# An encoder block in float32 on one core: the first two tiles side by side, first weights of a stage split earlier, first output products paired

## The chip, the cores and the metric

The kernel runs on one core of a Trainium2 chip. A core has TensorE (PE in the profile: matrix products into PSUM banks of 128 x 512 float32), VectorE (DVE), ScalarE (ACT), GpSimd (POOL), and SyncE (SP), which here issues the transfers between the chip's memory and SBUF. The engines run their instructions each in its own order and wait for one another through semaphores. The metric is the device time of one execution in microseconds, lower is better.

## The reference

One layer of a bidirectional encoder for two groups of sequences, 512 and 2048 tokens of width 1024, with 16 meta tokens in front of each:

```python
def mixer_layer(h, norm_g, w_in, na_rpb, sink, w_proj_a, w_proj_b, w_out, t5_bias):
    u = rms_norm(h, norm_g)
    proj = u @ w_in
    qa, ka, va, za, qb, kb, vb, zb, ga, gb = jnp.split(proj, cuts, axis=-1)
    o_a = neighbourhood_attention(qa, ka, va, na_rpb, n)
    o_b = window_attention(qb, kb, vb, t5_bias, sink, n)
    y_a = (o_a * jax.nn.silu(za)) @ w_proj_a
    y_b = (o_b * jax.nn.silu(zb)) @ w_proj_b
    merged = jax.nn.sigmoid(ga) * y_a + jax.nn.sigmoid(gb) * y_b
    return merged @ w_out
...
    h = h + mixer_layer(h, ...)
    return rms_norm(h[:, N_META:], final_g)
```

Branch a attends to a neighbourhood on a grid of 64 columns (8 heads of 64), branch b to a window of 128 tokens to either side (8 query heads, 2 key heads). Everything is float32.

## The kernel before

The 2560 tokens are five windows of 512: window 0 is the short sequence, 1 to 4 the long one. Activations lie feature-major, 128 features by 512 tokens to a tile. A float32 operand is split in a high and a low part (`split_part`: ACT copies the high part, then DVE or POOL subtracts for the low one), and a product is three products of parts (`mm3`, L135 to L137). Which engine makes the low part of weights is set by `lo_eng`: DVE in the first stages, POOL during attention.

The input projection has 42 output tiles of 128 features and 8 tiles of input (KT = 8), so 24 products to a tile and window. It runs in stages:

1. `beside(firsts, ...)`: the last window alone, 18 tiles one after another. `alone` runs one tile, `project` its products, with a yield after every six. `prep_last` first loads this window's x in four transfers of two tiles, scales it by the norm's weight (u, high part on ACT at L313, low on DVE at L314), squares it (L316) and adds up the squares (rs, L318 and L321). Its next step, which makes the reciprocal root, is called at the 9th and 14th yield. Meanwhile `prep_first` prepares windows 0 and 1, by a list of yields at which its steps are called (its sums rsp at L402, fin_v at L407).
2. `pass_(0, ...)` with `pairs`: windows 0 and 1 together, two tiles of weights at a time, by a scheme with seven products instead of eight (L758).
3. `beside(rest, ...)`: further tiles of the last window alone.
4. `pass_(2, ...)`: windows 2 and 3 as in 2.
5. Attention. Each window has 32 units of branch a, then 16 of branch b (`unit_a`, `unit_b`), cut into steps by yields. A b unit handles two heads: scores s, maximum, exponentials prs, normalising, transposes tp, products with v (ob). Between the steps TensorE's order is filled up with dense steps of six products by `fill`, with an account (`due`) that says how many are owed. The dense work of a window, in this order: `dense_pa` (psa, from y of branch a), `dense_pb` (psb, from y of branch b), `dense_out` (the output projection of w_o, whose results are hT), `dense_fin` (the final norm's factor rbs, and hT times rbs on POOL, L1239). psb of window w comes in the a units of window w + 1.
6. `finish_end`, for the last window: psb in pairs of tiles, then eight blocks of output (pse, tokens on the partitions, four blocks for either half of the columns), residual, final norm.

y of branch b for the last two head pairs of a window: each ob has its second half copied by ACT (L1140, ol), DVE adds the halves (L1143), POOL multiplies by z (L1146), ACT and POOL split the result in yb's high and low part (L959, L960). In the last window DVE stands in for POOL here. Of the four parts k = 0 to 3 of yb, 2 and 3 come from the last units.

A weight tile is loaded by `fetch_w` (512 KB, wraw) and split by `split_w` (wt), each from a pool of two buffers. TensorE's order is that of the program in the code (`manual_schedule`), and SP's in stages 1 to 4 and 6; on the other engines a scheduler decides, and `issue_after(x)` keeps an instruction behind x. At the start of stage 3 and of attention the first weights are fetched and split when the stage before has been written out:

```python
    w0 = start_w(rest)
    raws, wts = next(w0)
...
    lo_eng[0] = nc.gpsimd
...
    weights = Weights(srcs)
```

Of the kernel before, what the change touches and what calls it, by code (L numbers as in the profile page):

```python
# [17 lines left out]
P = 128  # L18
# [69 lines left out]
def encoder_block(ctx: ExitStack, tc: tile.TileContext, xT, x_end, w_in, w_pa, w_pb, w_o, norm_g, final_g,  # L88
# [86 lines left out]
    lo_eng, low = [nc.vector], [None]  # L175
# [9 lines left out]
    def split_part(h, l, r, eng=None):  # L185
        nc.scalar.copy(h, r)  # L186
        low[0] = (eng or lo_eng[0]).tensor_sub(l, r, f32(h)).ins  # L187
# [108 lines left out]
    def prep_last(meta):  # L296
# [5 lines left out]
        rs = us[w][2]  # L302
        for k in range(0, KT, 2):
            rows = xT[k * P : (k + 2) * P]
            xt = ev.tile([P, 2, WTOK], F32, tag="ev", name="xt")
            move(xt, rows[:, w * WTOK : (w + 1) * WTOK].rearrange("(k p) t -> p k t", p=P))
            if meta and k == 0:
                xm = st.tile([P, KT, N_META], F32, tag="xm", name="xm", bufs=1)
                move(xm, xT[:, TOK:].rearrange("(k p) t -> p k t", p=P))
            for j in range(2):  # L310
                g = ng[:, k + j : k + j + 1]
                h = uh[:, k + j, :WTOK]
                nc.scalar.mul(h, xt[:, j, :], g)  # L313
                nc.vector.scalar_tensor_tensor(ul[:, k + j, :WTOK], xt[:, j, :], g, f32(h), ALU.mult, ALU.subtract)  # L314
            if meta:
                nc.scalar.activation(xt, xt, AF.Square)  # L316
                if k == 0:
                    nc.vector.tensor_add(rs[:, :WTOK], xt[:, 0, :], xt[:, 1, :])  # L318
                else:
                    for j in range(2):  # L320
                        nc.vector.tensor_add(rs[:, :WTOK], rs[:, :WTOK], xt[:, j, :])  # L321
        if not meta:
            return
        t = ev.tile([P, WTOK], F32, tag="t", name="xms", bufs=3)
# [51 lines left out]
    def prep_first(sp, wa, loaded):  # L376
# [37 lines left out]
        for i in range(2):  # L414
            nc.scalar.copy(rss[i], spread(ps_t, "vt", dgs[i], P, 4))
# [260 lines left out]
    def alone(f, wt, held):  # L676
# [105 lines left out]
    def pairs(pp, wa, wb, fs, a, x, raw1, ahead, at):  # L782
# [19 lines left out]
        for j, (f1, f2) in enumerate(fs):  # L802
# [9 lines left out]
            step(j, 1)  # L812
            product(a, x["p6"], u[2], False)
# [25 lines left out]
    def beside(fs, raws, wts, own, wa, steps, at):  # L839
# [4 lines left out]
        ws = [*fs, *both[0]]  # L844
        lag[0] = 4
# [3 lines left out]
        for i, f in enumerate(fs):  # L849
# [4 lines left out]
            for _ in alone(f, wts[i], held):  # L854
# [38 lines left out]
    def pass_(wa, a, first, raw1, ahead, extra):  # L893
        with ExitStack() as pp:
            pool = [pp.enter_context(tc.tile_pool(name=f"p{i}", bufs=1, reuse_waits="tile")) for i in range(3)]
            return pairs(pool, wa, wa + 1, both, a, first.send(pool[2]), raw1, ahead, extra)

    w0 = start_w(firsts)
    raws, wts = next(w0)
    own = prep_last(True)  # L900
    next(own)
    with tc.tile_pool(name="sp", bufs=1, reuse_waits="tile") as sp:
        loaded = []
        steps = prep_first(sp, 0, loaded)
        next(w0)
        next(steps)
        next(w0)
# [277 lines left out]
    def dense_pb(w):  # L1185
        yh, yl = ys["b", w]
        acc["m", w] = []
        for f in range(KT):
            if f % 2 == 0:
                wt = weights.next()  # L1190
            sg = gated("sgb", g_d["b", w, f])
            ps = ps_d.tile([P, WTOK], F32, tag="d", name="psb")
            for k in range(4):
                s = slice((4 * (f % 2) + k) * P, (4 * (f % 2) + k + 1) * P)
                mm3(ps, wt[:, 0, s], wt[:, 1, s], yh[:, k, :], yl[:, k, :], k == 0, k == 3)
                if k % 2:
                    yield
# [341 lines left out]
```

## Time and profile before

| | before |
|---|---|
| median of 3 runs | 1918.05 us (1917.32 to 1919.04) |
| the profiled execution | 1917.62 us |
| its span | 1915.5 us |
| TensorE busy | 1882.1 us (98%) |
| VectorE, ScalarE, GpSimd busy | 69%, 60%, 38% |
| granted TensorE clock, mean | 0.997 |

Times within the profile are microseconds from the span's start. A group's or timeline's row has the engine, the line, the operation, what it writes and reads, the shape, and in square brackets the idle time of that engine before it with what ended it. The releaser is inferred from semaphores: where several are waited for, it is the one that came last.

### The profile page before, as it was taken

The page shows a single profiled execution, that of the slowest core. Times are in us where ns is not written, and L with a number is a line of the kernel's source. Part 1 is how long each engine was busy: PE and PEld are TensorE (multiplying, and loading weights), DVE is VectorE, ACT ScalarE, POOL GpSimd, SP SyncE. Part 2 cuts the span into 40 slices and gives each one's busy share as a digit, 9 for nine tenths or more (in the row PEclk, how much of TensorE's full clock was granted, in tenths as well). Part 3 has the DMA queues.
Part 4 walks back from the last instruction along what each step waited for, and adds up shares of the span by engine and source line. Part 5 has one row for each costly group of instructions (what it writes and reads, how often), then busy time and mean ns, then how long its engine had stood idle before and what let it go on. Part 6 is the DMA issues. An engine that isn't in the chain of part 4 may idle for free.

```text
span 1915.5 us, 29776 instructions
## 1 busy us (share of the span) xinstructions
PE 1882.1 (98%) x9925; PEld 1599.7 (84%) x9925; DVE 1313.5 (69%) x2899; ACT 1143.5 (60%) x2515; POOL 727.4 (38%) x556
## 2 busy tenths in 40 slices
PE   8999999999999999999999999999999999999998
PEld 6998888888878888888878888888888888888876
DVE  8886445556477544345457788878888887888874
ACT  6454444444464444444456787787788778778831
POOL 2005342323102222323223336646744864684320
PEclk9999999999999999999999999999999999999999
DMA  7667554644296775544369868977986996798482
GB/s 261 218 190 294 175 200 164 220 170 171 90 338 216 240 209 192 193 139 158 110 204 293 255 213 258 303 217 256 306 268 197 305 317 200 234 287 253 129 321 86
DMA packets 223761, 423.78 MB, mean 221 GB/s; under 512 B 49640, under 2 KB 90808, under 8 KB 222072
## 3 DMA queue, kind: packets, MB, share of 16 engines
q1 hardware_dynamic: 223320, 421.88, 67.1%
q8 instruction: 79, 1.29, 0.3%
q14 instruction: 74, 0.61, 0.1%
q10 hardware_dynamic: 288, 0.01, 0.0%
HBM read 303.07 MB, written 118.74 MB: 220 GB/s over the span
## 4 chain that ended last, share of the span: by engine, by line
PE 82%; DVE 5%; ACT 5%; DMA 4%; issue 2%; POOL 1%; SPq 0%; ACTq 0%; DVEq 0%; POOLq 0%
PE pa L758 23%; PE pe L758 11%; PE pc L758 6%; PE mm L137 3%; PE mm L135 3%; PE mm L136 3%; PE tp L1009 3%; PE pso L137 3%; PE pso L135 3%; PE pso L136 2%; PE tp L1109 2%; PE psb L136 2%; PE psb L137 1%; PE oa L1026 1%; PE psb L135 1%
## 5 line engine op out<-in xcount | busy, mean ns | idle before, releaser
L187 POOL TENSOR_TENSOR wt<-wraw,wt 128x512 fp32r<-128x512 f32 x164 | 213.8, 1323 | 271.5 <-ACT wt L186 260.9
L758 PE MATMUL pa<-u,wt 128*128 128x512 f32 x1008 | 242.9, 390 | 0.0
L758 PE MATMUL pa<-u,x 128*128 128x512 f32 x984 | 237.8, 390 | 0.0
L758 PEld LDWEIGHTS pa<-u,wt 128*128 128x128 f32 x1008 | 188.7, 188 | 39.0
L758 PEld LDWEIGHTS pa<-u,x 128*128 128x128 f32 x984 | 183.8, 188 | 38.1
L186 ACT CAST wt<-wraw 128x512 fp32r<-128x512 f32 x312 | 177.6, 618 | 54.9 <-PE mm L137 31.4
L729 POOL TENSOR_TENSOR s<-wraw,raw 128x512 f32<-128x512 f32 x40 | 57.9, 1446 | 273.9 <-DVE x L187 273.9
L135 PE MATMUL mm<-u,wt 128*128 128x512 f32 (+2 forms) x416 | 151.7, 365 | 8.3 <-ACT u L313 7.2
L724 POOL TENSOR_TENSOR s<-raw 128x512 f32<-128x512 f32 x40 | 58.6, 1466 | 255.1 <-DMA raw<-in_w_in_dram 137.6
L137 PE MATMUL mm<-u,wt 128*128 128x512 f32 (+2 forms) x416 | 148.0, 356 | 2.6 <-DVE wt L187 2.0
L136 PE MATMUL mm<-u,wt 128*128 128x512 f32 (+2 forms) x416 | 147.5, 354 | 0.0
L187 DVE TENSOR_TENSOR wt<-wraw,wt 128x512 fp32r<-128x512 f32 x148 | 103.5, 738 | 52.8 <-ACT wt L186 52.4
L758 PE MATMUL pe<-u,wt 128*128 128x512 f32 x504 | 121.8, 391 | 0.0
L758 PE MATMUL pc<-u,wt 128*128 128x512 f32 x504 | 121.1, 389 | 0.0
L1013 DVE TENSOR_TENSOR pl<-tp,ph 128x512 fp32r<-128x512 f32 (+7 forms) x160 | 99.0, 619 | 30.4 <-ACT ph L1012 28.7
L942 ACT ACTIVATE pr<-s,nm 128x384 f32<-128x384 f32 (+5 forms) x160 | 91.2, 570 | 41.2 <-DVE nm L935 40.3
L758 PE MATMUL pe<-u,x 128*128 128x512 f32 x480 | 115.3, 389 | 0.0
L758 PEld LDWEIGHTS pc<-u,wt 128*128 128x128 f32 x504 | 94.6, 188 | 19.6
L758 PEld LDWEIGHTS pe<-u,wt 128*128 128x128 f32 x504 | 94.2, 188 | 19.4
L737 POOL TENSOR_TENSOR s<-wraw,s 128x512 f32<-128x512 f32 x40 | 52.5, 1312 | 145.8 <-DVE wt L187 145.8
L135 PE MATMUL pso<-mh,wt 128*128 128x512 f32 x256 | 107.8, 421 | 0.0
L758 PEld LDWEIGHTS pe<-u,x 128*128 128x128 f32 x480 | 90.1, 188 | 18.7
(237 smaller groups left out, 5035.8 us busy)
## 6 DMA issues: line engine op xcount, KB each, us to landing
wraw<-in_w_in_dram SPq DMA_DIRECT2D x86, 512.0 KB
qa<-evq SPq DMA_DIRECT2D x20, 1024.0 KB
raw<-in_w_in_dram SPq DMA_DIRECT2D x40, 512.0 KB
q<-qa SPq DMA_DIRECT2D x20, 1024.0 KB
wraw<-in_w_o_dram SPq DMA_DIRECT2D x32, 512.0 KB
kbt<-kb SPq DMA_DIRECT2D x32, 384.0 KB
qb<-evq SPq DMA_DIRECT2D x20, 512.0 KB
ka<-evk SPq DMA_DIRECT2D x20, 512.0 KB
```

The source lines that it names most:

```text
L135: nc.tensor.matmul(ps, wh, uh, start=first, stop=False)
L136: nc.tensor.matmul(ps, wh, ul, start=False, stop=False)
L137: nc.tensor.matmul(ps, wl, uh, start=False, stop=last)
L186: nc.scalar.copy(h, r)
L187: low[0] = (eng or lo_eng[0]).tensor_sub(l, r, f32(h)).ins
L724: eng.tensor_add(s1, a21, a22)
L729: eng.tensor_sub(s3, a11, a21)
L737: eng.tensor_sub(s4, a12, s2)
L758: nc.tensor.matmul(ps, wt[:, a, s], u[:, b, kk, :], start=first and kk == 0 and i == 0, stop=kk == 3 and i == 2, skip_group_check=True)
L942: nc.scalar.activation(out, s, AF.Exp, bias=nm, scale=-1.0, accum_out=sm)
L1009: nc.tensor.transpose(tp[:kb, i * P : (i + 1) * P], pr[:, b * kb : (b + 1) * kb], ident)
L1013: nc.vector.tensor_sub(pl_[:kb, a], tb, f32(ph_[:kb, a]))
```

## The change

The opening: nine products of ones with ones stand ahead on TensorE. The first two tiles' weights come in halves (256 KB each), the first two x tiles in two transfers, and the two tiles run side by side in steps of six products, in the order 0,1,0,1,0,0,1,1. The squares of x and their sums come behind all scalings, the meta tokens' transfer last. The steps of the norm move from the 9th and 14th to the 10th and 15th yield, and the list for windows 0 and 1 changes. What stores a tile's result (`store`) is issued behind the next weights' low part, two copies behind their high part.

Stage starts: `pairs` calls `opening` in the last pair of a pass, which fetches and splits the first weights of what follows.

Attention: `unit_b` yields between its two heads, so both heads' scores stand in two steps; for a window's first b unit the loop calls `fill(1)` between them. `dense_pb` runs its first two output tiles as a pair, k = 0, 1 of both, then k = 2, 3 of both.

End: two blocks of pse are opened with k = 0 to 5 of both, then k = 6, 7 of each; in the last window `dense_fin` is woven in behind one step of `dense_pa` instead of three.

SP in the opening, before (wraw are weights, xt the last window's x, xm the meta tokens, x0 and x1 those of windows 0 and 1):

```order
L131 DMA wraw_280<-in_w_in_dram 128x1024
L131 DMA xt_290<-in_xT_dram 128x2x512
L131 DMA xm_292<-in_xT_dram 128x8x16
L131 DMA xt_300<-in_xT_dram 128x2x512
L131 DMA xt_309<-in_xT_dram 128x2x512
L131 DMA xt_318<-in_xT_dram 128x2x512
L131 DMA wraw_338<-in_w_in_dram 128x1024
L131 DMA wraw_340<-in_w_in_dram 128x1024
L131 DMA x0_345<-in_xT_dram 128x2x512 x2
L131 DMA x1_346<-in_xT_dram 128x2x512 x2
```

and with the change:

```order
L131 DMA wraw_290<-in_w_in_dram 128x512
L131 DMA xt_300<-in_xT_dram 128x512 x2
L131 DMA wraw_292<-in_w_in_dram 128x512
L131 DMA xt_310<-in_xT_dram 128x2x512
L131 DMA wraw_290<-in_w_in_dram 128x512
L131 DMA wraw_292<-in_w_in_dram 128x512
L131 DMA xt_322<-in_xT_dram 128x2x512
L131 DMA xt_328<-in_xT_dram 128x2x512
L131 DMA xm_334<-in_xT_dram 128x8x16
L131 DMA wraw_339<-in_w_in_dram 128x1024
L131 DMA x0_344<-in_xT_dram 128x2x512 x2
```

The weights of tile 0 and 1 and the first x come in halves, in turn, tile 1's weights ahead of the last two x transfers, and the third tile's weights stand where the second's were.

TensorE where window 3's b units end and window 4's a units begin, before (ob is the last of y's inputs; s and tp are scores and transposes of an a unit):

```order
L1133 MATMUL ob_17931<-ph_8389,vb_17012 128x256
L1138 MATMUL ob_17931<-pl_8390,vb_17012 64x256
L1133 MATMUL ob_17931<-ph_8389,vb_17012 128x256
L1136 MATMUL ob_17931<-pms1_8442,vms_8443 64x128 x2
L1138 MATMUL ob_17931<-pl_8390,vb_17012 64x256
L997 MATMUL s_17947<-kd_17612,q_17610 128x312
L998 MATMUL s_17947<-kd_17612,q_17610 128x312
L1009 MATMUL tp_17958<-ident_243,pr_17830 104x128 x4
L135 MATMUL psa_17971<-ya03_15877,wt_17728 128x512
```

and with the change, from the same ob on:

```order
L1201 MATMUL ob_17994<-ph_8411,vb_17064 128x256
L1206 MATMUL ob_17994<-pl_8412,vb_17064 64x256
L1201 MATMUL ob_17994<-ph_8411,vb_17064 128x256
L1204 MATMUL ob_17994<-pms1_8455,vms_8456 64x128 x2
L1206 MATMUL ob_17994<-pl_8412,vb_17064 64x256
L1063 MATMUL s_18010<-kd_17666,q_17664 128x312
L1064 MATMUL s_18010<-kd_17666,q_17664 128x312
L1075 MATMUL tp_18021<-ident_243,pr_17892 104x128 x4
L135 MATMUL psb_17972<-yb03_17351,wt_17797 128x512
```

The dense step behind the transposes was the first of a tile of psa; now it is psb with k = 2 and 3, which reads the y that this ob ends. POOL at the same place, before:

```order
L1239 TENSOR_TENSOR hT_17125<-hT_17125,rbs_17773 128x512
L1239 TENSOR_TENSOR hT_17264<-hT_17264,rbs_17773 128x512
L1239 TENSOR_TENSOR hT_17413<-hT_17413,rbs_17773 128x512
L1146 TENSOR_TENSOR y32_17163<-y32_17163,z_17303 128x512
L1146 TENSOR_TENSOR y32_17223<-y32_17223,z_17371 128x512
L960 TENSOR_TENSOR yb13_17300<-y32_17163,yb03_17299 128x512
L187 TENSOR_TENSOR wt_18034<-wraw_17864,wt_18034 128x512 x2
L960 TENSOR_TENSOR yb13_17300<-y32_17223,yb03_17299 128x512
```

and with the change:

```order
L1311 TENSOR_TENSOR hT_17030<-hT_17030,rbs_17697 128x512
L1311 TENSOR_TENSOR hT_17177<-hT_17177,rbs_17697 128x512
L1311 TENSOR_TENSOR hT_17316<-hT_17316,rbs_17697 128x512
L187 TENSOR_TENSOR wt_17965<-wraw_17795,wt_17965 128x512 x2
L1214 TENSOR_TENSOR y32_17215<-y32_17215,z_17355 128x512
L1026 TENSOR_TENSOR yb13_17352<-y32_17215,yb03_17351 128x512
L1214 TENSOR_TENSOR y32_17275<-y32_17275,z_17428 128x512
L1026 TENSOR_TENSOR yb13_17352<-y32_17275,yb03_17351 128x512
```

The low half of a weight tile (wt) stood between the two low parts of yb, and stands ahead of both products now.

TensorE at the end of the last window's units, before:

```order
L1133 MATMUL ob_20216<-ph_8389,vb_19359 128x256
L1138 MATMUL ob_20216<-pl_8390,vb_19359 64x256
L1133 MATMUL ob_20216<-ph_8389,vb_19359 128x256
L1136 MATMUL ob_20216<-pms1_8442,vms_8443 64x128 x2
L1138 MATMUL ob_20216<-pl_8390,vb_19359 64x256
L135 MATMUL psa_20209<-ya04_18245,wt_20107 128x512
```

and with the change:

```order
L1201 MATMUL ob_20262<-ph_8411,vb_19432 128x256
L1206 MATMUL ob_20262<-pl_8412,vb_19432 64x256
L1201 MATMUL ob_20262<-ph_8411,vb_19432 128x256
L1204 MATMUL ob_20262<-pms1_8455,vms_8456 64x128 x2
L1206 MATMUL ob_20262<-pl_8412,vb_19432 64x256
L135 MATMUL psb_20301<-yb04_19711,wt_20168 128x512
L136 MATMUL psb_20301<-yb14_19712,wt_20168 128x512
```

Behind the last ob stood the rest of psa, then psb; now psb with k = 2 and 3 follows at once.

The diff, cut to its core:

```diff
@@ split_part
-        nc.scalar.copy(h, r)
+        high[0] = nc.scalar.copy(h, r).ins
@@ prep_last
+            for j, n in ((0, 1), (1, 1)) if meta and k == 0 else ((0, 2),):
+                move(xt[:, j : j + n], xT[(k + j) * P : (k + j + n) * P, w * WTOK : (w + 1) * WTOK]
+                     .rearrange("(k p) t -> p k t", p=P))
+            if between is not None:
+                next(between, None)
...
+        yield
+        for k, xt in enumerate(xts):
+            with tc.issue_after(scaled.ins):
+                nc.scalar.activation(xt, xt, AF.Square)
+            if k == 0:
+                nc.vector.tensor_add(rs[:, :WTOK], xt[:, 0, :], xt[:, 1, :])
+            else:
+                for j in range(2):
+                    nc.vector.tensor_add(rs[:, :WTOK], rs[:, :WTOK], xt[:, j, :])
@@ alone
-                store(f, w, ps, (mul, rs[:, :WTOK]))
+                with tc.issue_after(low[0]):
+                    store(f, w, ps, (mul, rs[:, :WTOK]))
@@ pairs
             step(j, 1)
+            if end:
+                opening()
@@ beside
+        def first_two():
+            gens = [alone(fs[i], wts[i], held) for i in range(2)]
+            for i in (0, 1, 0, 1, 0, 0, 1, 1):
+                next(gens[i])
+                yield
+            for g in gens:
+                finish(g)
@@ opening
+    def start_two(raws, wts):
...
+        fetch(0, lo)
+        part_of(0, lo)
+        yield
+        fetch(1, lo)
+        yield
+        part_of(1, lo)
+        yield
+        fetch(0, hi)
+        fetch(1, hi)
+        yield
+        part_of(0, hi)
+        part_of(1, hi)
+        yield
+
+    warm = ps_t.tile([P, WTOK], F32, tag="vt", name="warm")
+    for _ in range(9):
+        nc.tensor.matmul(warm[:, :P], ones, ones, start=True, stop=True)
...
-        begun = beside(firsts, raws, wts, (own, (9, 14)), 0, steps, [2, 20, 27, *(28 + 27 * i // 10 for i in range(16))])
+        begun = beside(firsts, raws, wts, (own, (10, 15)), 0, steps, [2, 27, 31, *(31 + 25 * i // 10 for i in range(16))])
...
+    finals = pass_(0, *begun, prep_ahead(2), dict(zip(steps[:-1], steps[:-1])), lambda: opened.extend(next(w0)))
...
+    def open_weights():
+        nonlocal weights
+        lo_eng[0] = nc.gpsimd
+        weights = Weights(srcs)
@@ unit_b
         for h in range(2):
+            if h:
+                yield
@@ dense_pb
+        for f, k0 in [(0, 0), (1, 0), (0, 2), (1, 2), *((f, k) for f in range(2, KT) for k in (0, 2))]:
@@ finish_end
+        ahead = [bank("pse") for _ in range(2)]
+        for b in range(2):
+            out(ahead[b], b, 0, range(KT - 2))
...
+                if ahead:
+                    ps = ahead.pop(0)
+                    out(ps, b, c, range(KT - 2, KT))
@@ phases
-            yield from islice(pa, 3)
+            yield from islice(pa, 3 if w < NWIN - 1 else 1)
@@ units
             if i + 2 < N:
                 next(units[i + 2][2])
+                if units[i + 2][0] == "b":
+                    if units[i + 1][0] == "a":
+                        fill(1)
+                    next(units[i + 2][2])
```

More of the change, by code (lines that the diff above doesn't have):

```diff
@@ L780, in begin, with pairs @@
         return a
-    def pairs(pp, wa, wb, fs, a, x, raw1, ahead, at):
+    def pairs(pp, wa, wb, fs, a, x, raw1, ahead, at, opening):
         u = us[wa]
@@ L853, in beside @@
                     raws.append(fetch_w(w_in[ws[i + 3]]))
-            for _ in alone(f, wts[i], held):
+            for _ in () if own is not None and i == 1 else first_two() if own is not None and i == 0 else \
+                    alone(f, wts[i], held):
                 q += 1
@@ L1369, in encoder_block @@
     ph_, pl_ = (at.tile([P, 14, P], F32R, tag=f"p{i}", name=f"p{i}", bufs=1) for i in "hl")
-    weights = Weights(srcs)
     next(units[0][2])
```

106 lines of the change are left out of this document (59 added, 47 removed).

## The prediction

> **What bounds the kernel now.** The page comes first, for the shares of the engines, then the waits of TensorE over the whole span.
>
> ```profile
> span 1915.5 us, 29776 instructions
> PE 1882.1 (98%) x9925; PEld 1599.7 (84%) x9925; DVE 1313.5 (69%) x2899; ACT 1143.5 (60%) x2515; POOL 727.4 (38%) x556
> ...
> PE mm L135 <- ACT u L313: 7.2, 1, 7.2
> PE psb L136 <- POOL yb L960: 4.0, 5, 1.7
> PE pse L1302 <- ACT mh L1289: 2.5, 1, 2.5
> PE s L1089 <- ACT prs L942: 2.1, 4, 0.6
> PE mm L137 <- DVE wt L187: 2.0, 3, 0.9
> PE psb L135 <- DVE ta L1183: 1.4, 1, 1.4
> ...
> PE s L1089 <- ACT pr L942: 0.5, 1, 0.5
> ```
>
> TensorE works 1882.1 of 1915.5 us and waits 33.4. The change removes no product and adds nine small idle ones, so its whole effect lies in those 33.4 us, plus stretches at a low clock. Each wait row names what TensorE waited for, the total, the count and the longest. The parts of the change answer to rows: the opening (7.2), the first weights of a stage (part of the 2.0, and rows shown further on), the scores of a b unit (2.1 and 0.5), the first psb products of a window (4.0), the end (1.4 and 2.5).
>
> **The opening.** The rows are from the timeline: start, duration, engine, line, and in brackets the idle time before and who ended it. The last is a window of one microsecond: behind the engines stand the granted clock, the DMA share and GB/s.
>
> ```profile
> 4.42 1.14 ACT L186 CAST wt<-wraw 128x512 fp32r<-128x512 f32 x2 [1.75 <-DMA wraw<-in_w_in_dram]
> 6.45 1.34 ACT L313 ACTIVATE u<-xt,ng 128x512 fp32r<-128x512 f32 x2 [0.89 <-DMA xt<-in_xT_dram]
> 7.20 1.42 DVE L314 SCALAR_TENSOR_TENSOR u<-xt,ng,u 128x512 fp32r<-128x512 f32 x2 [0.24 <-ACT u L313]
> 7.22 0.80 PE L135 MATMUL mm<-u,wt 128*128 128x512 f32 x1 [7.22 <-ACT u L313]
> 11.48 1.04 ACT L316 ACTIVATE xt<-xt 128x1024 f32<-128x1024 f32 x1
> 12.44 0.63 PE L137 MATMUL mm<-u,wt 128*128 128x512 f32 x1
> 12.87 0.47 PE L135 MATMUL mm<-u,wt 128*128 128x512 f32 x1
> 20.82 0.39 PE L136 MATMUL mm<-u,wt 128*128 128x512 f32 x1
> 21.04 0.39 PE L137 MATMUL mm<-u,wt 128*128 128x512 f32 x1
> 31.82 1.48 PE L171 MATMUL rs_rb<-rs_dg,ones 128*128 128x128 f32 x10 [1.09 <-DVE rs_dg L163]
> ...
> 7.00:8.00 1.00, 0.78 (x1) 0.29 (x1) 0.80 (x2) 1.00 (x4) 0.00 (x0) 1.00 1.06 391
> ```
>
> Before, 512 KB of weights land at 4.42, then 512 KB of x, and the first product starts at 7.22. It runs cold, 0.43 us apart (12.44 to 12.87), then 0.23 apart (20.82 to 21.04), and the first two tiles' 48 products end at 21.3. At 391 GB/s 256 KB take 0.67 us. Half a tile of weights therefore lands near 3.7, the first x rows near 4.4, and their scaling (half of 1.34) ends near 5.2: the first product comes 2 us earlier. The two tiles need 3 MB in all, 8 us at that rate, so the last x rows land near 11.3; two scalings (1.34) and the low parts (0.7 behind them) give 13.4, and three steps of six products (18 x 0.23 = 4.1) close both tiles near 17.5. The third tile's weights stand on ACT behind four squares: 12.7 + 4 x 1.04 + a cast of 0.57 is 17.5, and with the low part the tile starts at 18.2 against 21.3. **Term: -3.1.** The nine idle products have the form of those at 31.82, ten in 1.48 us: 1.3 us, perhaps 2.7 at the low clock, from about 1 us on, so they are done by 4 and cost nothing. If they do not warm TensorE, the two tiles lose little, because they wait for x until 13.4; bounds -4.5 and +0.5, the latter if the squares and sums, now behind all scalings, come late. I take the worked value.
>
> **First weights of the second and third stage.**
>
> ```profile
> 535.55 0.50 PE L137 MATMUL mm<-u,wt 128*128 128x512 f32 x1 [0.25 <-DVE wt L187]
> 552.57 0.50 PE L135 MATMUL mm<-u,wt 128*128 128x512 f32 x1 [0.82 <-ACT wt L186]
> 576.29 0.50 PE L137 MATMUL mm<-u,wt 128*128 128x512 f32 x1 [0.93 <-DVE wt L187]
> 986.59 0.50 PE L135 MATMUL mm<-u,wt 128*128 128x512 f32 x1 [0.26 <-ACT wt L186]
> 987.94 0.50 PE L137 MATMUL mm<-u,wt 128*128 128x512 f32 x1 [0.62 <-POOL wt L187]
> ```
>
> The first fetch now precedes four x transfers on SP and the split is done in the last pair of products, which TensorE covers. Of the first three waits (2.0) I take 1.7, since the third lies well inside the stage: **-1.7** (bounds 0 and -2.0). The last two (0.88) should go with their split: **-0.8** (0 to -0.9). Moved past the x transfers, each fetch delays them by 1.34 us; nothing reads those rows until the stage begins, and a late one would eat the gain, hence the bound 0.
>
> **Scores of the b units.** The five waits of 0.5 us (2.1 and 0.5 in the waits) fall where a window's first b unit puts two pairs of score products on two banks at once. The added dense step between them is 6 products, 1.4 us, more than any of the five. **-2.3** (-1.5 to -2.6).
>
> **The first psb products of a window** pay for that step: dense work runs one step ahead more in every window. The end of y's chain is ACT's copy, DVE's sums, POOL's product, ACT's cast and POOL's low part.
>
> ```profile
> 1165.57 1.28 POOL L1146 TENSOR_TENSOR y<-y,z 128x512 f32<-128x512 f32 x1 [1.07 <-DVE y L1143]
> 1166.88 0.62 ACT L959 CAST yb<-y 128x512 fp32r<-128x512 f32 x1
> 1167.58 1.29 POOL L960 TENSOR_TENSOR yb<-y,yb 128x512 fp32r<-128x512 f32 x1 [0.73 <-ACT yb L959]
> ...
> 1326.55 5.31 POOL L1239 TENSOR_TENSOR hT<-hT,rbs 128x512 f32<-128x512 f32 x4
> 1328.87 0.37 ACT L1140 COPY ol<-ob 64x256 f32<-64x256 f32 x1 [0.63 <-PE ob L1138]
> 1329.85 0.57 DVE L1143 TENSOR_TENSOR y<-ob,ol 64x128 f32<-64x128 f32 x2
> 1331.81 2.67 POOL L1146 TENSOR_TENSOR y<-y,z 128x512 f32<-128x512 f32 x2
> 1338.38 0.50 PE L136 MATMUL psb<-yb,wt 128*128 128x512 f32 x1 [0.88 <-POOL yb L960]
> 1339.63 0.50 PE L136 MATMUL psb<-yb,wt 128*128 128x512 f32 x1 [0.28 <-POOL yb L960]
> ...
> 1679.72 0.50 PE L136 MATMUL psb<-yb,wt 128*128 128x512 f32 x1 [1.72 <-POOL yb L960]
> ```
>
> From the copy's start (1328.87) to the sums' end (1330.42) are 1.6 us, then 1.28, 0.62 and 1.29 with handoffs of 0.1 to 0.4: about 5.5 us from the last ob to yb's low part if POOL is free. Before, three dense steps lie between; now three, two, one and none after windows 0 to 3, the pairing of the first two outputs already counted. After window 3 the cover is one a unit's scores and transposes (1.2 us) and four psb products (0.9): 5.5 - 2.1 = 3.4 of waiting, against 1.72. After window 2 a step of 1.4 lies between, 2.0, with some queue 2.2; after window 1 the queue decides: products are wanted about 2.1 us earlier (a step and the attention beside it) and POOL's y, late by the hT products until 1331.86, can start 1.3 earlier, so the waits of that window, 0.88 and 0.28 more, become 2.0. Behind a waiting psb stand the next a units' scores on TensorE, and their exponentials on ACT start as much later. Sum 7.6 against 4.0: **+3.6**. Bounds: 0, because the hT products come a step earlier too and the weights' low half changes place with y on POOL; +12.6 if POOL doesn't move (below).
>
> **The end.**
>
> ```profile
> 1828.92 1.30 DVE L1146 TENSOR_TENSOR y<-y,z 128x512 f32<-128x512 f32 x1
> ...
> 1866.00:1868.00 2.00, 2.00 (x6) 1.57 (x6) 0.62 (x2) 0.00 (x0) 0.00 (x0) 0.62 1.00 401
> 1868.00:1870.00 2.00, 2.00 (x6) 1.55 (x5) 0.00 (x0) 0.00 (x0) 0.00 (x0) 0.53 1.03 412
> ```
>
> The wait of 2.5 at pse came behind 18 products; now 36 stand there, 4.1 us more, so it goes. The 1.4 (a bank held by ta) gives way to y's chain of the last unit, which nothing covers any more: copy 0.37, sums 0.57, product about 0.7 on a DVE free of POOL's hT (it took 1.30 beside them), cast and low part 0.6 each, handoffs, less the psb products that need only the other y: 3.0. Against 3.9: **-0.9** (+1.5 to -2.0). The windows show the clock at 0.62 and 0.53 for the 4 us behind the wait of 2.5: 12 products where 17 would fit at 0.23, about 1.55 us lost. After the change that stretch goes, and two gaps of about 3 us (window 3, the end) may each bring one; at even odds that is zero.
>
> [...]
>
> **Sum.** -3.1 - 1.7 - 0.8 - 2.3 + 3.6 - 0.9 = -5.2, from 1917.62 (the profiled execution, 2.12 of it outside the span, 0.43 below the median 1918.05): **1912.4**.
>
> **Rivals.**
>
> *POOL's backlog stays put (slower).* The hT products are held behind the split of the next weights, so dense work may run ahead while they don't. Then y is no earlier and the psb products are wanted 1, 2 and 3 steps of 2.1 us sooner: +12.6 instead of +3.6, and cold clock after two gaps, +3.1: 1917.62 - 8.8 + 15.7 = 1924.5. It decides from 8.8 us of added waiting there. For it: hT until 1331.86 is what held y at 1331.81. Against: in the new order the same products stand further ahead of y. 6%.
>
> *The boundaries are free (faster).* POOL's free share (38% busy) absorbs the steps, the waits there stay 4.0, the cold stretch isn't replaced: -8.8 - 1.55, 1907.3. For it: the weights' low half no longer stands between the two low parts after window 3. Against: the unqueued chain alone exceeds the cover. 20%.
>
> *The opening does not gain.*
>
> ```profile
> 16.31 1.42 DVE L321 TENSOR_TENSOR rs<-rs,xt 128x512 f32<-128x512 f32 x2
> 18.85 3.48 DVE L321 TENSOR_TENSOR rs<-rs,xt 128x512 f32<-128x512 f32 x2
> ```
>
> Two sums take 1.42 alone and 3.48 beside POOL's adds. All seven now come late: at 1.74 each instead of 0.71 that is 7 us, in front of the low parts of the third and fourth tile's weights. The 3.1 would go: 1915.5. Against: the squares, which feed the sums, come one per 1.04 us, so DVE has gaps for the weights. 20%. [...]
>
> **How the numbers follow.** The forecast has 52% (its own range 1910 to 1914.9), the slower rival 6%, the faster 20%, the third 20%, others 2%. A measurement of this kernel can tell about 0.2% from no change: 1914.2 and 1921.9 are the bounds. Faster: 20 and most of 52, 0.64; same: 20, the rest and the others, 0.30; slower: 0.06. For eight in ten the range takes in the third rival and nearly all of the faster one, 1906.7 to 1916.5, and leaves out the slower.
>
> **What would show it.** First real product at 5.2 and third tile at 18.2; no wait above 0.2 us for wt near 535, 552 and 987; no waits of s products; psb waits of 2.0, 2.2 and 3.4 after windows 1 to 3; one wait of some 3 us before the last psb products and none at pse. It would be wrong if psb waits sum above 12, or the third tile starts after 20.

## The result, and the profile after

The change is slower: 1940.35 us (median of four runs, 1938.02 to 1942.71) against 1918.55 us, a ratio of 1.0114 with a 95% interval of 1.0097 to 1.0132. The profiled execution took 1939.76 us. The forecast was 1912.4, faster.

The page of the changed kernel, and TensorE's waits over its whole span (who waits, for whom, us in total, times, longest):

```profile
span 1937.6 us, 29796 instructions
PE 1892.0 (98%) x9943; PEld 1604.8 (83%) x9943; DVE 1322.4 (68%) x2897; ACT 1144.9 (59%) x2515; POOL 729.6 (38%) x558
...
PE mm L135 <- ACT wt L186: 4.7, 2, 4.4
PE s L1157 <- ACT prs L1008: 3.8, 4, 1.4
PE psb L135 <- ACT yb L1025: 3.7, 4, 1.7
PE ob L1201 <- DVE y L1211: 3.3, 6, 1.1
PE pa L769 <- ACT wt L186: 3.2, 1, 3.2
PE psb L136 <- POOL yb L1026: 2.8, 3, 1.6
PE pa L769 <- DVE wt L187: 2.3, 1, 2.3
PE rs_rb L171 <- DVE rs_dg L163: 2.3, 1, 2.3
...
PE mm L135 <- ACT u L315: 0.6, 1, 0.6
```

The wait of 7.2 us at the start is gone, as meant (0.6 is left behind the idle products). But TensorE idles 45.6 us instead of 33.4, at places that were not in the list before: the eighth tile's weights (4.4 of the 4.7), the first pair's weights (3.2 and 2.3), ob, and scores that wait longer. It is also busy 9.9 us longer, of which the nine idle products are 4.1; the rest I put down to the low clock (ahead of the last product 0.50 for 23.9 us in all, before the change for 6.8).

Since every product of the projection and every score product has its counterpart in the other kernel, the two timelines can be laid side by side. The table gives a product's start in either, and how late the change is:

| product | before | after | late by |
|---|---|---|---|
| first product of the sixth tile | 43.70 | 41.25 | -2.5 |
| last product of the seventh tile | 57.86 | 53.72 | -4.1 |
| last product of the ninth tile | 67.47 | 70.72 | +3.3 |
| second pair of weights | 150.79 | 162.12 | +11.3 |
| first score of window 0, branch a | 993.07 | 1001.08 | +8.0 |
| first score of branch b, window 0 | 1082.61 | 1088.93 | +6.3 |
| last score of branch b, window 0 | 1150.36 | 1160.62 | +10.3 |
| last score of branch b, window 2 | 1479.94 | 1494.40 | +14.5 |
| last score of branch b, window 4 | 1814.22 | 1843.83 | +29.6 |
| last product | 1906.59 | 1928.40 | +21.8 |

So there are three stretches. The opening is 2.5 us ahead at the sixth tile, not far from the forecast 3.1, and 4.1 at the end of the seventh, of which 1.7 is a low clock that only the kernel before has there (0.60 from 44 to 48 us, 1.00 after the change; see the last section); by 150 us it is 11.3 late. The stage starts and window 0's first units win back 5.0. Attention and the end lose 15.5. (Of the 29.6, some 7 us are five dense steps of 1.4 that are only done earlier.)

What stood in the way in the opening: the transfers' issue on SP, ACT's cast of the eighth tile's weights, and TensorE, first after, then the issue of that transfer before.

```profile
41.37 2.69 SPq L131 DMA_DIRECT2D qa<-evq  x3
48.81 1.11 SPq L131 DMA_DIRECT2D wraw<-in_w_in_dram  x1
57.82 1.14 ACT L186 CAST wt<-wraw 128x512 fp32r<-128x512 f32 x2 [8.73 <-DMA wraw<-in_w_in_dram]
18.61 0.50 PE L135 MATMUL mm<-u,wt 128*128 128x512 f32 x1 [0.35 <-ACT wt L186]
58.49 0.79 PE L135 MATMUL mm<-u,wt 128*128 128x512 f32 x1 [4.37 <-ACT wt L186]
```

```profile
40.60 2.70 SPq L131 DMA_DIRECT2D qa<-evq  x3
45.49 1.34 SPq L131 DMA_DIRECT2D wraw<-in_w_in_dram  x1
```

The third tile starts at 18.61 (forecast 18.2). But the eighth tile's weights stand on SP behind four stores of q (1 MB each; the row has three, the fourth is issued at 48.20). They are issued at 48.81 instead of 45.49, and are cast at 57.82. In the kernel before they stand behind the same four stores, but go out 3.3 us earlier, and TensorE comes to that tile only at 58.09. With the change it is done with the seventh tile 4.1 us earlier, waits 4.37 us, and then runs cold (clock 0.50 from 56.14 to 62.97, products 0.43 us apart). The second loss, after and then before: ACT and TensorE at the first pair of weights.

```profile
132.36 4.26 ACT L368 CAST u<-x 128x512 fp32r<-128x512 f32 x8
136.52 1.14 ACT L186 CAST wt<-s 128x512 fp32r<-128x512 f32 x2
137.71 0.93 PE L769 MATMUL pa<-u,wt 128*128 128x512 f32 x2 [3.15 <-ACT wt L186]
140.98 3.35 PE L769 MATMUL pa<-u,wt 128*128 128x512 f32 x7 [2.34 <-DVE wt L187]
```

```profile
125.86 0.62 ACT L186 CAST wt<-s 128x512 fp32r<-128x512 f32 x1 [3.89 <-PE mm L137]
127.00 0.62 ACT L186 CAST wt<-s 128x512 fp32r<-128x512 f32 x1 [0.52 <-DVE s L725]
129.10 4.26 ACT L360 CAST u<-x 128x512 fp32r<-128x512 f32 x8
```

Eight casts of x operands, which nobody needs yet, stood behind the casts of the pair's weights, and stand ahead of them now. And in attention, the first b units of window 4 on TensorE after the change:

```profile
1767.11 0.39 PE L135 MATMUL pso<-mh,wt 128*128 128x512 f32 x1
...
1768.49 0.35 PE L1157 MATMUL s<-kbt,q 128*128 128x402 f32 x1
...
1771.48 0.45 PE L1157 MATMUL s<-kbt,q 128*128 128x402 f32 x1 [1.06 <-ACT prs L1008]
...
1774.71 0.45 PE L1157 MATMUL s<-kbt,q 128*128 128x402 f32 x1 [1.40 <-ACT prs L1008]
...
1775.18 0.39 PE L135 MATMUL pso<-mh,wt 128*128 128x512 f32 x1
```

The added dense step (pso at 1767.11) stands between the first two heads. The kernel before has no wait there in this window: its wait of 0.56 us, at 1751.17, is in the third unit (the first unit's scores begin at 1743.78). But between 1768.49 and 1775.18 there is no dense step at all, where before one stood at each unit, and two waits of over 1 us stand in the second and third unit. The program's order shows it as well; the sequence on TensorE from that place, with the number of products (scores of one head are s x2, a dense step is pso x6):

```
before: s x2, s x2, tp, pso x6, oa x6, s x2, s x2, tp, pso x6, oa x4, s x2, s x2, tp, pso x6
after:  s x2, pso x6, s x2, tp, oa x6, s x2, s x2, tp, oa x4, s x2, s x2, pso x12, tp, pso x6
```

Counted in front of each score product, the change's dense work is ahead of the kernel before by one step from the b units of window 0 on, by two from those of window 1 on, and so on to five in window 4, but for single units where it falls back for a while. The code places the first b units' scores two units ahead, while the account still draws on the a units' supply. Here that supply is used up; two steps come at once (pso x12) when that of the b units opens.

### The profile page after: what moved, and what is told of

Its sections match the earlier page's. It is cut to its first block, busy times and chain, and to the rows that moved or that the text cites. A ratio compares the mean times of both kernels' runs of the same rounds, so it can differ in the third digit from the quotient of the medians.

```text
span 1937.6 us, 29796 instructions
## 1 busy us (share of the span) xinstructions
PE 1892.0 (98%) x9943; PEld 1604.8 (83%) x9943; DVE 1322.4 (68%) x2897; ACT 1144.9 (59%) x2515; POOL 729.6 (38%) x558
## 4 chain that ended last, share of the span: by engine, by line
PE 78%; DVE 9%; ACT 6%; DMA 3%; issue 2%; POOL 2%; SPq 0%; ACTq 0%; DVEq 0%; POOLq 0%
PE pa L769 23%; PE pe L769 11%; PE pc L769 6%; PE mm L135 4%; PE mm L137 4%; PE mm L136 4%; PE pso L137 3%; PE pso L135 3%; PE pso L136 2%; PE tp L1075 2%; DVE s L1001 1%; PE tp L1177 1%; PE oa L1092 1%; PE oa L1090 1%; PE psb L136 1%
## 5 line engine op out<-in xcount | busy, mean ns | idle before, releaser
L1008 ACT ACTIVATE prs<-s,nm 128x402 f32<-128x402 f32 (+1 forms) x160 | 91.4, 573 | 32.9 <-DVE nm L1001 29.4
```

The lines of the kernel that those rows point to most:

```text
L1008: nc.scalar.activation(out, s, AF.Exp, bias=nm, scale=-1.0, accum_out=sm)
```

## The experiments

All times are medians; the ratio is to the kernel before, with its 95% interval. As the kernel before was between 1916.7 and 1918.55 in the different groups of runs, differences are taken between ratios (0.001 is 1.9 us).

| run | what | us | ratio |
|---|---|---|---|
| e1 | the change without the added step | 1927.68 | 1.0050 (1.0035 to 1.0066) |
| e2 | the change with the old opening | 1930.69 | 1.0064 (1.0048 to 1.0080) |
| e3 | before, with early weights | 1915.08 | 0.9986 (0.9975 to 0.9998) |
| e4 | e1 and e2 together | 1918.07 | 0.9999 (0.9987 to 1.0010) |
| e5 | e1, held stores later | 1922.71 | 1.0020 (1.0007 to 1.0034) |
| e6 | e1, old list from 28 on | 1921.44 | 1.0022 (1.0010 to 1.0035) |
| e7 | e5 and e6 together | 1916.49 | 0.9987 (0.9977 to 0.9997) |
| e8 | e3 with the reordered end | 1908.29 | 0.9948 (0.9936 to 0.9961) |
| e9 | e8 with the psb pair | 1916.60 | 0.9995 (0.9986 to 1.0005) |
| e10 | e9 with four gate buffers | 1911.24 | 0.9972 (0.9961 to 0.9983) |
| e11 | e8, a step moved between the heads | 1909.27 | 0.9955 (0.9942 to 0.9969) |
| e12 | e8 with the mended opening | 1910.95 | 0.9963 (0.9951 to 0.9976) |
| e13 | the change, step moved, not added | 1926.16 | 1.0046 (1.0030 to 1.0061) |
| e14 | e8, dense work one step behind | 1907.87 | 0.9947 (0.9934 to 0.9959) |
| e15 | e8, two steps behind | 1912.62 | 0.9981 (0.9973 to 0.9990) |

### The added step, the opening, the early weights

e1 takes out one line pair:

```diff
-                    if units[i + 1][0] == "a":
-                        fill(1)
```

> The change as it is, but without the one dense step owed more between the two heads of a window's first b unit (fill(1)); the yield between the heads stays. In the change the loss from the first b unit of window 0 to the end is 15.5 us against before. Theory (supply): each phase has a fixed number of dense steps, so a step done early is missing at the end of the phase, where score, ob and psb products then stand bare; without fill(1) those waits fall back to what they were before, and the time to 1924 to 1928. Rival (order): the yield between the heads has reordered ACT and DVE, and that costs; then the time stays above 1935. My prediction's account (one step less cover at each boundary only, 3.6 us) would give 1936 to 1937.

Measured: 1927.68. Against the change that is 0.0064 less, 12.3 us: the supply theory's range, far from the 3.6 of the prediction. In its profile no wait for ob and none of psb for yb is left, and the scores wait 2.6 us as before the change; the waits of the transposes rise from 1.5 to 7.9 (e9 tells why). Idle time is 6.0 us less than in the change's profile and busy time 5.5, which I put down to the clock (mean 0.995, and 0.993 in the change).

e2 puts the old opening back:

```diff
-    w0 = start_two(raws, wts)
-    next(w0)
-    own = prep_last(True, w0)
+    w0 = start_w(firsts)
+    raws, wts = next(w0)
+    own = prep_last(True)
...
-        begun = beside(firsts, raws, wts, (own, (10, 15)), 0, steps, [2, 27, 31, *(31 + 25 * i // 10 for i in range(16))])
+        begun = beside(firsts, raws, wts, (own, (9, 14)), 0, steps, [2, 20, 27, *(28 + 27 * i // 10 for i in range(16))])
```

> The change with its opening undone (two tiles one after another, whole loads, squares beside scalings, the old list of steps, stores and copies not held back, no idle products); everything behind it as in the change. ACT's and DVE's order in attention is then that of the change. Theory (opening): the 11.3 us by which the change is late from 150 us on are made in the opening alone, by weights that land behind the stores of q at 58 us and by a late preparation of windows 0 and 1; all of it comes back, 1928 to 1930, and TensorE waits neither at 58 nor at 137 us. Rival: part of it comes from what stands behind (the first pair's weights), then over 1932.

Measured: 1930.69, 0.0050 or 9.6 us less than the change, a little short of the 10.5 to 12.5 expected. In its profile the products start within 0.1 us of those before from 50 to 535 us, and the waits at 58 and 137 are gone, so all of the 11.3 was made there. Why the time fell one to two us less than that was not followed up.

e3 is the kernel before with one part of the change:

```diff
             step(j, 1)
+            if end:
+                opening()
...
+    finals = pass_(0, *begun, prep_ahead(2), dict(zip(steps[:-1], steps[:-1])), lambda: opened.extend(next(w0)))
...
+    finals = pass_(2, *begun, prep_end(), [(j + (i != 1), i) for j in range(2 * KT) for i in (1, 0, 2)], open_weights)
```

> The kernel before with only the first weights of the second and third stage fetched and split in the last pair of the pass ahead. In the change the shift against before falls by 5.0 us over these two places (11.33 to 8.33, then to 6.33). Theory: the part stands by itself and brings 5.0, 1913 to 1914. Rival: part of the 5.0 is only slack that DVE and ACT make up because they were late there; then my term of 2.5, 1915 to 1917.

Measured: 0.9986, 2.7 us less: the rival, and the size that the prediction gave this part (2.5). The timelines show why the 5.0 was too much. The change wins 4.7 us up to 989 us, and so does e8 below, which has this part and no new opening. Right behind, TensorE waits for the low part of u (1.49 us at 992.03 in e3), which the kernel before does not do, and by the first score of attention e8 has given 2.2 back.

e4 joins the edits of e1 and e2.

> The change with the opening undone and without fill(1) (both edits of the two kernels ahead). Theory: both losses are separate and add up, 1940.35 - 11.3 - 13 to 15.5 = 1913.5 to 1916. Rival (they hide behind one another): above 1920.

Measured: 0.9999, or 21.9 us less than the change; the two edits alone give 12.3 and 9.6. They add up. But the time is that of the kernel before, above the 1913.5 to 1916 expected: what remains of the change (early weights, pairing, end) should have gained, and doesn't. e8 and e9 find out why.

### Inside the opening

e5 holds the stores of q back for two yields more, so that the eighth tile's weights pass them on SP:

```diff
-                    if q == own[1][-1]:
-                        for fn in held[1]:
-                            fn()
-                        held[1] = None
+                if own is not None and q == 17:
+                    for fn in held[1]:
+                        fn()
+                    held[1] = None
```

> The change without fill(1), and the four held stores of q issued two yields later, so that the eighth tile's weights stand ahead of them on SP. Without it the shift against before is +10.9 us at 150 us (a wait of 4.8 at 58 us with a cold clock behind it, then waits of 3.2 and 2.1 at 137 with another). Theory (weights behind the stores): the wait at 58 goes with its cold stretch, about 6 us, 1921 to 1923; the waits at 137 stay. Rival (the transfers are the bound there, whatever their order): the wait comes at one of the next tiles, over 1925.

e6 changes the list of yields:

```diff
-[2, 27, 31, *(31 + 25 * i // 10 for i in range(16))]
+[2, 27, 28, *(28 + 27 * i // 10 for i in range(16))]
```

> The change without fill(1), and in the list of yields at which windows 0 and 1 are prepared the entries behind the second set as before (28 + 27i/10, from 28 on, in place of 31 + 25i/10). ACT then casts the first pair's weights ahead of the eight last x operands, as before the change, and not behind them. Theory (order): the waits at 137 us go with their cold stretch, about 8 us, 1919 to 1921; the wait at 58 stays. Rival (the preparation as a whole is late, DVE being full from 70 to 130 us): the waits at 137 stay in other places, over 1924.

e7 has both.

> Both edits of the two kernels ahead. Theory: they add up, and what is left of the side-by-side opening is a gain of 2 to 3 us at 150 us: 1912 to 1915. Rival: the start's gain has nothing to go to, since transfers and DVE set the pace until the pairs begin; then the shift at 150 us is 0 or above, 1916 to 1918.

Measured against e1: e5 5.8 us less, e6 5.4, e7 12.1. In e5's profile no wait is left at 58 us and those at 134 and 137 stay, as expected. e6 went another way than I wrote: the time at 58 us was saved, because a step of the preparation now runs where TensorE waited (rs_rb, at 54.96 in place of 64.81), and of the later waits a part stayed:

```profile
131.51 0.85 PE L769 MATMUL pa<-u,wt 128*128 128x512 f32 x2 [2.63 <-ACT wt L186]
133.50 4.63 PE L769 MATMUL pa<-u,wt 128*128 128x512 f32 x10 [1.13 <-DVE wt L187]
```

In e6's order one half of the pair's weights stands ahead of the u operands on ACT and DVE, the other still behind; in e7 and before both stand ahead, and neither waits; in the change both stand behind. So the two waits are shown to be the two orders: weights behind stores on SP, and weights behind operands on ACT and DVE. With both mended the opening is 1.2 us ahead at 150 us (149.63 against 150.79), instead of 11.3 late.

### The end, the pairing, the gates

e8 adds the end of the change to e3:

```diff
+        ahead = [bank("pse") for _ in range(2)]
+        for b in range(2):
+            out(ahead[b], b, 0, range(KT - 2))
...
-            yield from islice(pa, 3)
+            yield from islice(pa, 3 if w < NWIN - 1 else 1)
```

> The kernel before with the first weights of the stages split early and the end reordered (two blocks of pse opened ahead, the final norm of window 3 woven in two steps earlier); no other part of the change. Theory: TensorE's waits at the end (1.4 and 2.5) and the cold stretch behind them go, 4 to 5.5 us less than with the early weights alone, 1909.5 to 1911.5. Rival (my term of 0.9, a new wait for y's chain in place of the old ones): 1914 to 1915.

Measured: 0.9948, 7.3 us less than e3, more than both expectations. Laid beside the kernel before, e8 wins 6.1 us behind the last score: the two waits of 1.4 and 2.5 and 1.7 us of a low clock (0.50 for 3.41 us, from 1866.46 in the kernel before) make 5.6 of it. Where the rest comes from was not followed up; the runs of e3 spread from 1910 to 1921. Its waits hold neither pse nor ta any more, and the psb waits are as before:

```profile
PE psb L136 <- POOL yb L983: 4.1, 5, 1.7
PE s L1112 <- ACT prs L965: 2.1, 4, 0.6
```

e9 adds the pairing of the first two psb tiles, e10 a fourth buffer for the gate tiles:

```diff
+        for f, k0 in [(0, 0), (1, 0), (0, 2), (1, 2), *((f, k) for f in range(2, KT) for k in (0, 2))]:
...
-        t = pools["d"].tile([P, WTOK], F32, tag="sg", name=name, bufs=3)
+        t = pools["d"].tile([P, WTOK], F32, tag="sg", name=name, bufs=4)
```

> The kernel with the early weights and the reordered end (1908.3), and with it the pairing of the first two psb tiles; no yield in the b units, no step more. Theory (gate tiles): the psb waits for yb (4.0) go, but the third and fourth tile's gates come late through a ring of three buffers, DVE stands on a gate's transfer and the a units' transposes wait for pr: 4 to 10 us more, 1912 to 1918. Rival (the yield between the heads was what cost those 10 us): 1903 to 1906.

> As the kernel with the pairing, but with four buffers for the gate tiles in place of three (at the end four of them and two of the other pool, so that the memory suffices). Theory (gate tiles): neither psb nor tp waits, 4 us less than without the pairing, 1903.5 to 1905.5. Rival (DVE is held by the bunched work of two tiles, not by a transfer): the tp waits stay and the time is that of the three buffers, 1912 or more.

Measured: the pairing costs 0.0047, 9.0 us. Waits in e9, DVE in e4 (which has the same pairing), and waits in e10:

```profile
PE tp L1032 <- DVE pr L976: 7.6, 12, 1.5
```

```profile
1355.48 0.69 DVE L1227 TENSOR_TENSOR sgb<-psb,sgb 128x512 f32<-128x512 f32 x1 [3.24 <-DMA sgb<-gb]
1356.09 0.41 DVE L976 TENSOR_SCALAR pr<-pr,rd 128x384 f32<-128x384 f32 x1
1356.56 0.55 PE L1032 MATMUL tp<-ident,pr 128*128 128x128 f32 x3 [2.01 <-DVE pr L976]
```

```profile
PE tp L1032 <- DVE pr L976: 1.9, 7, 0.4
PE s L1112 <- issue: 1.6, 1, 1.6
PE s L1112 <- DMA kbt<-kbm: 1.3, 1, 1.3
```

The psb waits are gone in both. But in the paired order the fourth tile's gate is late (its ring has three buffers), DVE stands 3.24 us on its transfer (in e4) with pr's normalising behind it, and the transposes of the next a unit wait: 7.6 us in e9, in place of the 4.1 of psb in e8. A fourth buffer brings that to 1.9 and the time down by 4.4 us, so the ring is shown as the cause of about half. e10 still is 4.6 us above e8, not below it. Its profile has two waits that e8's has not, at the first score of b in windows 2 and 3: 1.3 for the transfer of b's keys, and 1.6 for which the profile names no releaser. Neither belongs to the pairing alone: e3, which has none, waits 1.7 us for the keys at the first of these places, and e12 0.7 and 1.2 at both. Whether they come from the order or from the chance of an execution was not settled.

### Moving the step instead of adding it

```diff
                         fill(1)
+                        due -= 1
```

> The early weights and the reordered end, no pairing, with the yield between the heads and the dense step between them, but with that step taken off the next owed amount (due - 1), so that it is moved and not added. Theory (supply): without a step more per window no phase runs out; the five score waits of 0.5 (2.6) go and nothing else moves, 1905 to 1907. Rival (moving a step only moves the wait, since ACT then has the same work in less time): 1908 to 1910.

> The change as it is, but the dense step between the two heads is taken off the next owed amount (due - 1): it is moved, not added, so dense work runs no step further ahead per window. Theory (supply): it is not the step between the heads that costs but that each phase is then short of a step at its end; the time falls to that without the step, 1926 to 1929 (the opening's 11 and the pairing's 8 stay). Rival (the step in that place disturbs ACT's and DVE's order): it stays above 1935.

e13, on the change itself, takes 13.0 us off, as much as leaving the step out (12.3). The step stands in the same place, between the same two heads; only the account is even. In e13 dense work is one step ahead of the kernel before only at the first b unit of each window, and level again behind it. So what cost was a lead that stays and grows from window to window, and that is shown. e11 gains nothing over e8 (0.9955 against 0.9948): the five score waits (in the first unit of window 0, in the third of the others) are replaced by five of up to 1.2 us in the second unit, which is the rival. The step between the heads was no remedy for these waits in either form.

e12 puts the mended opening under e8.

> The early weights and the reordered end, with the side-by-side opening in its mended form (held stores two yields later, the old list from 28 on). Theory: its shift at 150 us was -1.2 in the run with both mends, so 1906.5 to 1907.5. Rival: that gain is within the noise of the stores and of the cold stretch at 44 us, 1908 to 1910.

Measured: 0.9963, no gain over e8 (0.9948): the rival. Its timeline is 2.6 us ahead of e8's at 64 us, 1.7 of it because e8's profile has the low clock at 44 us (0.59 from 44 to 48), and 2.1 until 1400. Then it gives that back in windows 2 and 3: 0.9 and 0.7 for the keys of a (kd), 0.7 for a normalising on DVE (pr), and 0.7 and 1.2 at the first score of b, for which the profile names no releaser.

Two more turn the account the other way:

```diff
-        dense, key, due = iter(()), None, 0.0
+        dense, key, due = iter(()), None, -1.0
```

> The early weights and the reordered end (1908.3), and the account of dense steps begins at -1: the dense work lags one step behind in all windows, the contrary of the change. Theory (cover): every place where y or a score stands bare has one step more in front; of the psb waits (4.1) some 2 to 3 go, 1905 to 1907. Rival (the waits are set by POOL's and DVE's queues, which move with the step): 1908 to 1910.

> As the kernel ahead with the account at -2. Theory (cover): all psb waits go, 1904 to 1906. Rival: as the kernel ahead or slower, 1908 or more, because the late steps must be made up at the end of the window.

e14 is as fast as e8 (0.9947); its psb waits fall from 4.1 to 1.1, and 2.3 of tp and 2.5 of ob take their place. e15, with two steps behind, is 6.3 us slower than e8. So the cover theory has the place right, and the gain goes to other waits: the account stood at its best or within a step of it.

The fastest kernels are e8 and e14, 0.5% below the one before (0.9936 to 0.9961 and 0.9934 to 0.9959).

## Why the prediction was wrong

- **Opening, -3.1: the mechanism right, the term wrong.** Third tile at 18.6, first product at 5.8, products at 0.23 us from the start, the idle products out of the way by 5.2 (they took 4.1 us, not 1.3 to 2.7). What failed is the step from the third tile's start to the end of the stage. I carried 3.1 us through to the total as if nothing else set the pace up to 150 us. Then the transfers did, at 58, and ACT's and DVE's order, at 137. My third rival had the gain vanish through late sums, with a price of 0; the loss had other causes and came to 9.6 us. I had the list of yields in view and gave it no cost: the moved preparation has eight casts and eight subtractions, and the question was what they would stand ahead of. The order showed it. (In my row of 7 to 8 us the column of the clock says 1.00, although the products there stand 0.43 us apart. The trace's record of the clock begins at 13.03 us before the change and at 4.94 after it, and ahead of that the column shows 1.00. Only the spacing tells of the low clock there: from 59.08 to 62.49 after the change, where the record has 0.50, the products stand 0.43 us apart too.)
- **Stage starts, -2.5: the size right, not its make-up.** e3 gives 2.7. More was won at the weights, and some of it lost again in a wait for the low part of u, for which I had no term.
- **Scores, -2.3: wrong.** I put the five waits in each window's first b unit. Only that of window 0 (1083.54) is there; the other four are in the third unit, where the added step does not stand. Their waits rose from 2.6 to 3.8. In window 4 the step that was put between the first two heads was missing at the second and third unit.
- **psb after a window, +3.6: the place and the lead right, not the price.** I wrote 2.0, 2.2 and 3.4 after windows 1 to 3; the rows there show 1.3, 1.9 and 2.5:

```profile
1346.61 0.51 PE L135 MATMUL psb<-yb,wt 128*128 128x512 f32 x1 [0.42 <-ACT yb L1025]
1347.96 0.50 PE L136 MATMUL psb<-yb,wt 128*128 128x512 f32 x1 [0.85 <-POOL yb L1026]
1517.18 0.50 PE L136 MATMUL psb<-yb,wt 128*128 128x512 f32 x1 [1.63 <-POOL yb L1026]
1518.43 0.50 PE L136 MATMUL psb<-yb,wt 128*128 128x512 f32 x1 [0.28 <-POOL yb L1026]
1692.36 0.50 PE L135 MATMUL psb<-yb,wt 128*128 128x512 f32 x1 [1.67 <-ACT yb L1025]
1693.71 0.50 PE L136 MATMUL psb<-yb,wt 128*128 128x512 f32 x1 [0.85 <-DMA kd<-kam]
```

So cover was lost about as reckoned. What I overlooked is that a phase has a fixed number of dense steps, so a lead takes cover from everything at a window's end, and not only from psb. Into the 12.3 us of the added step went these 5.7 us, and beside them the waits of ob (3.3, 0.7, 0.6 and 0.4), 1.2 more of the scores, 1.5 more for a bank (ta), 2.0 of psb in the last window and the clock (0.50 for 3.41 us each from 1148.40, 1694.54 and 1865.20), less 6.4 of the transposes' waits that the lead takes away. In my first rival the price lay in POOL's queue; it needed 8.8 us of added waiting at these places to decide for it.
- **Pairing: counted at nothing.** I entered it only as one step of cover given back. It costs 9.0 us beside e8, about half of it through a ring of three gate tiles which I had named nowhere. In the change itself the added step hides part of it (the transposes wait 1.5 us there, 7.9 without the step); the change without the pairing was not tried.
- **End, -0.9: too small.** e8 gives 7.3 where the dense work doesn't run ahead. I had the new waits eat up the old ones, which they do in the change: 0.5 and 0.2, then 1.1 and 0.2 before the last psb products, against a forecast of 3.0, and none at pse.
- **Clock: zero by even odds.** After the change there are cold stretches (clock 0.50) at 56, 138, 1148, 1694 and 1865 us, 23.9 us in all, in place of two (44 and 1866 us), 6.8 in all. The 1.55 us that I gave to one of them does not follow from my row (12 products at 0.23 leave 1.2 of 4 us); 3.41 us at half the clock are 1.7. It entered no term of the sum.

By differences of ratios the parts come to: opening 9.6, added step 12.3, pairing 9.0, yield between the heads 0.8 (e4 less e9, within the intervals), early weights -2.7, end -7.3. Their sum is 21.7, against 21.9 measured. Four of them are steps along one chain of kernels (before, e3, e8, e9, e4), which add up by themselves; what the sum tests is that the opening and the step add up. That the pairing, the yield and the end weigh the same inside the change is not shown.

## What to carry to other kernels

Where work is dealt out from a fixed supply to cover waits, ask of an extra helping where it will be missing: lay the two orders side by side through the end of the phase, not only at the place of the edit. A gain at the start reaches the end only if nothing behind it sets the pace (here transfers that stand behind stores on SP, and the order of two engines behind a moved list), and a pairing doubles what its ring buffers have to hold. Of a bundle of seven edits two carried a gain of 10 us, and three hid it.

## What the runs showed of the hardware

The low clock came behind less idling than I reckoned with. After the change it fell behind a single wait of 1.74 us (clock, third from the end, DMA share and GB/s behind it):

```profile
1148.45 0.79 PE L135 MATMUL psa<-ya,wt 128*128 128x512 f32 x1 [1.74 <-DVE ta L1251]
...
1148.00:1152.00 4.00, 3.55 (x11) 2.87 (x12) 3.55 (x11) 0.69 (x3) 0.40 (x1) 0.57 0.63 188
```

A wait of 1.72 us before the change left it at 1.00 (at 1679.72), and so did one of 2.27 us after it (at 32.89), so in these traces the length alone does not decide.

In the traces' records of the clock, before and after the change, each such stretch ahead of the last product is 3.41 or 6.83 us long, at 0.50: 3.41 from 43.75 and 1866.46 before, 6.83 from 56.14 and 138.06 and 3.41 from 1148.40, 1694.54 and 1865.20 after.

It also fell with no wait of TensorE over 0.24 us close ahead: from 44 to 48 us in the kernel before, not in e4, which has the same opening (0.60 and 1.00).

```profile
44.00:48.00 4.00, 4.00 (x12) 3.14 (x12) 3.66 (x17) 0.00 (x0) 0.00 (x0) 0.60 1.03 406
```

```profile
44.00:48.00 4.00, 4.00 (x19) 3.28 (x18) 3.66 (x17) 0.00 (x0) 0.00 (x0) 1.00 1.03 406
```

In both TensorE is busy throughout, twelve products in the one and nineteen in the other, and behind it e4 is 1.6 us ahead. Two microseconds earlier stand sixteen products of one column each (fin_v, 41.92). That these are the reason wasn't tried. Of the profiled executions with the old opening, before, e2, e3, e8, e9 and e15 have the stretch, e4, e10, e11 and e14 have not, so a single profile of this kernel may be some 1.7 us off for that alone (3.41 us at 0.50).
